# Output projection, residual and router by blocks of columns with the samples in them, smaller first weight tiles, and a new order of the work ahead of them, in a one-layer decoder step

## The chip, the cores and the metric

The kernel runs on one core of one Trainium2 chip. The metric is the device time of one execution in microseconds (us); three runs of the kernel before have a median of 1264.1 us. Engines are named as in the profile: PE is TensorE, DVE VectorE, ACT ScalarE, POOL GpSimd; SP only issues transfers (DMA).

## The reference

One layer of a decoder for a prompt of 256 tokens and 8 sample sequences of one token each, width 1024, everything in fp32:

```python
sh1, sc1, g1, sh2, sc2, g2 = jnp.split(jax.nn.silu(c) @ ada_w + ada_b, 6, axis=-1)
h = rms_norm(x, norm1_w) * (1.0 + sc1[:, None]) + sh1[:, None]
z = h @ w_in
...
x = x + g1[:, None] * (jnp.concatenate([ret_out, att_out], axis=-1) @ w_out)
h = rms_norm(x, norm2_w) * (1.0 + sc2[:, None]) + sh2[:, None]
ff = moe(h.reshape(B * T, D), router_w, router_b, w_gate_up, b_gate_up, w_down, b_down).reshape(B, T, D)
x = x + g2[:, None] * ff
```

`ret_out` is a retention (linear attention) group of 8 heads, `att_out` a sparse attention of 8 heads, which for the samples gathers the 256 best of 1024 cached keys and values. `moe` has 32 experts, of which each token takes the best 4; an expert is a gate-up matrix of 1024 x 2048, a clamped SwiGLU and a down matrix of 1024 x 1024, 12.58 MB in fp32. All 32 are read once, 402.7 MB.

## The kernel before

The program is one stream, in which a scheduler orders the instructions of every engine by the priority of the segment that they stand in: `seg("name")` opens a segment, and the table `PRIO` gives each name an offset. Pools of tiles add waits where a buffer is used again.

Ahead of the experts come: the conditioning (`ada`, six parts of 1024 columns, from `ada_w`), the input projection (`zblock`, blocks of 512 columns of `w_in`), the attention of the samples in two passes of four samples (`sample_attention(0)` and `(1)`: gathers of keys by POOL, scores by DVE, gathers of values by POOL (L895), probabilities times values on PE (L965), and the fold into `mixT` through L972 and L973), the retention, and then the output projection. `mixT` (128 x 8 x 288) holds the mixed heads with the width on the partitions; columns 0 to 255 are the prompt, 256 to 263 the samples.

The output projection `out_proj(c, k0)` makes, for a chunk `c` of 128 tokens, two blocks of 128 x 512 in two halves of the sum (`k0` is 4, then 0): 64 matmul instructions in all at L1277 (an fp32 matmul is two instructions in the profile), each block followed on DVE by a product with `g1b` (L1279) and a sum into `x` (L1280). The samples have matmuls of their own (L1285). After its projection a chunk is normed by `norm2(c)`: transposes into `xT` (which is `mixT`) and squares on ACT; then `router(c)`: 8 logit matmuls (L1353), the choice of the best 4 on DVE, and `ranks(c)`, each token's place among an expert's. Chunk 0 goes through this while PE still projects chunk 1. `keep_warm` puts 11 bf16 matmuls of no use (L1345) into the pauses of that stretch. `gather_in` (L1391) then collects the tokens of the first pair of experts by one-hot matmuls, DVE scales them (L1402), and expert 0 begins (gate-up L1581, transposes L1514, down L1591, scatter L1525).

Weights come through a ring of tiles, filled by SP in the order of use as tiles come free: 7 tiles of 2 MB (`ring2`), 4 of 1 MB (`ringp`), and, once `mixT` and its neighbours are free, one of 2 and one of 1 MB, 21 MB in all. The four tiles of `ringp` hold `w_out` (4 MB) first. So all but the last 7 MB of the ring is filled while the mixing still runs, and tile n of the second round is requested when the first round's tile n has been read. The first tile of the ring is thus freed by expert 0's first quarter.

Of the kernel before, what the change touches and what calls it, by code (L numbers as in the profile page):

```python
# [1793 lines left out]
```

## Time and profile before

| | us |
|---|---|
| median of three runs (1260.33, 1264.1, 1264.23) | 1264.1 |
| the profiled execution, its own time | 1260.99 |
| its span in the trace | 1259.2 |
| PE busy | 1171.8 (93%) |
| DVE busy | 488.6 (39%) |
| first matmul of the output projection's main part (L1277) | at 300.26 |
| first matmul of expert 0 (L1581) | at 347.27 |

The span is 1.8 us shorter than that execution's time. Times within the span count from its start. [...] In a timeline a bracket behind a group tells how long the engine was idle before it and what ended that.

### The profile page before, as it was taken

The numbers are of one execution on the slowest core, as the hardware profiler recorded it, in microseconds if no ns is written. First come the engines' busy times: TensorE is split into PE (matmuls) and PEld (weight loads), VectorE is DVE, ScalarE is ACT, GpSimd is POOL, SyncE is SP. The second block draws the span as 40 slices with busy tenths as digits, with TensorE's granted clock in tenths as the row PEclk, the third lists the DMA queues.
The fourth block names the chain that finished last, engine by engine and source line by source line (L and its number), as shares of the span: only waits on it lengthen the run. The fifth ranks groups of instructions, "written<-read, shape, count | busy, mean of one in ns | idle before, by whom it ended". The sixth has DMA issues, their size and how long they took to land. (4 is left out here: it accounts for less than half of the span.)

```text
span 1259.2 us, 14226 instructions
## 1 busy us (share of the span) xinstructions
PE 1171.8 (93%) x5672; PEld 467.3 (37%) x5673; DVE 488.6 (39%) x1171; ACT 134.5 (11%) x289; POOL 138.8 (11%) x221
## 2 busy tenths in 40 slices
PE   7999978889999999999999898989999898998998
PEld 3443333356533334333343333333333333333332
DVE  3239865436534233332333233232323232333243
ACT  1222112211210000000000000000000000000000
POOL 3402273340010000000000000000000000000000
PEclk8999999999999999999999999999999999999999
DMA  9636896757779999999999999999999999999997
GB/s 379 269 128 237 301 367 227 233 191 305 321 292 428 427 430 428 428 430 426 430 428 430 430 426 429 431 428 428 431 428 429 430 427 431 428 429 406 427 428 313
DMA packets 53350, 475.81 MB, mean 378 GB/s; under 512 B 6896, under 2 KB 7568, under 8 KB 15520
## 3 DMA queue, kind: packets, MB, share of 16 engines
q1 hardware_dynamic: 45472, 454.04, 86.2%
q0 software_dynamic: 4432, 13.74, 3.0%
q10 hardware_dynamic: 3376, 7.09, 1.8%
q8 instruction: 46, 0.75, 0.2%
q14 instruction: 24, 0.20, 0.0%
HBM read 470.69 MB, written 4.11 MB: 377 GB/s over the span
## 5 line engine op out<-in xcount | busy, mean ns | idle before, releaser
L1581 PE MATMUL pg<-w,xg 128*64 128x512 f32 x2048 | 470.6, 600 | 35.2 <-DMA w<-lay_w_exp 33.7
L1581 PEld LDWEIGHTS pg<-w,xg 128*64 128x64 f32 x2048 | 140.7, 137 | 322.0 <-issue 267.3
L1591 PE MATMUL py<-w,sg 128*64 128x512 f32 x1024 | 236.0, 602 | 11.9 <-DMA w<-lay_w_exp 11.4
L1555 DVE TENSOR_TENSOR hb<-pt,biasT 128x512 f32<-128x512 f32 x64 | 44.3, 692 | 358.9 <-PE pt L1514 350.2
L1540 POOL TENSOR_SCALAR og<-kp,rankm,comb 128x64 f32<-128x64 f32 (+1 forms) x64 | 36.9, 593 | 848.9 <-PE pz L1525 794.6
L1591 PEld LDWEIGHTS py<-w,sg 128*64 128x64 f32 x1024 | 71.0, 138 | 146.9 <-issue 129.7
L1547 ACT ACTIVATE hs<-pg 128x512 f32<-128x512 f32 x64 | 38.2, 597 | 614.5 <-PE pg L1581 614.5
L538 PE MATMUL acc<-w,hT 128*128 128x512 f32 x208 | 102.3, 623 | 0.0
L1598 DVE TENSOR_TENSOR ys<-py,g2n 64x512 f32<-64x512 f32 x62 | 42.7, 688 | 113.3 <-PE py L1591 112.6
L1525 PE MATMUL pz<-ys,og 128*128 128x512 f32 (+1 forms) x136 | 67.8, 630 | 1.6 <-DVE ys L1594 0.8
L1528 DVE TENSOR_TENSOR x<-x,pz 128x512 f32<-128x512 f32 x68 | 46.5, 688 | 58.2 <-PE pz L1525 58.2
L1391 PE MATMUL pz<-oh,hn 128*128 128x112 f32 x480 | 58.1, 274 | 0.0
L1391 PEld LDWEIGHTS pz<-oh,hn 128*128 128x128 f32 x480 | 56.0, 192 | 0.0
L538 PEld LDWEIGHTS acc<-w,hT 128*128 128x128 f32 x208 | 37.5, 196 | 42.5 <-issue 40.6
L1560 ACT ACTIVATE sg<-hb 128x256 f32<-128x256 f32 x64 | 26.7, 416 | 224.9 <-DVE hb L1559 224.9
L1514 PEld LDWEIGHTS pt<-ident,hs 128*128 128x128 f32 x256 | 27.0, 141 | 53.2 <-issue 53.2
L1514 PE MATMUL pt<-ident,hs 128*128 128x128 f32 x256 | 42.2, 287 | 0.0
L1525 PEld LDWEIGHTS pz<-ys,og 128*128 128x128 f32 (+1 forms) x136 | 23.1, 192 | 46.0 <-issue 29.6
L1577 DVE COPY og<-pt 128x256 f32<-128x256 f32 (+1 forms) x17 | 7.2, 424 | 63.8 <-PE pt L1514 63.8
L1563 DVE TENSOR_TENSOR sg<-sg,hb 128x256 f32<-128x256 f32 x64 | 26.9, 420 | 3.9 <-DVE hb L1562 0.5
L1562 DVE SCALAR_TENSOR_TENSOR hb<-hb 128x256 f32<-128x256 f32 x64 | 27.2, 425 | 2.2
L316 PE MATMUL acc<-w,cT 128*32 128x512 f32 x128 | 24.9, 609 | 0.5 <-ACT t L848 0.5
(461 smaller groups left out, 849.5 us busy)
## 6 DMA issues: line engine op xcount, KB each, us to landing
w<-lay_w_exp SPq DMA_DIRECT2D x130, 2048.0 KB, 28.1
w<-lay_w_exp SPq DMA_DIRECT2D x122, 1024.0 KB, 26.9
w<-lay_ada_w SPq DMA_DIRECT2D x20, 1024.0 KB, 10.9
w<-lay_w_in SPq DMA_DIRECT2D x15, 1024.0 KB, 6.5
w<-lay_w_out SPq DMA_DIRECT2D x4, 1024.0 KB, 5.4
s<-qd ACTq DMA_DIRECT2D x4, 512.0 KB, 7.8
w<-lay_w_exp SPq DMA_DIRECT2D x4, 512.0 KB, 14.8
hT<-lay_x SPq DMA_DIRECT2D x1, 1152.0 KB
```

The source lines that it names most:

```text
L538: T.matmul(pc[c], hT[:, k, 128 * c:128 * c + 128], w[k], start=(k == 0), stop=(k == 7))
L1391: put(T.matmul(px[:, k, :n, 8:64], hn[:, c, 512 * g + 128 * k:512 * g + 128 * k + 128], oh, start=(c == 0 and k == 0), stop=(c == 1 and k ...
L1514: on_pe(T.transpose(out, in_, ident[:k, :k]))
L1525: on_pe(T.matmul(pz[n], gT[i, 128 * c:128 * c + 128], ys[i, o:o + 512], start=True, stop=True))
L1528: V.tensor_add(x[:, c, sl], x[:, c, sl], pz[n])
L1540: G.tensor_scalar(og[:, c, js], iota2[:, 0:js.stop - js.start], rank(c), gate(c), op0=ALU.is_equal, op1=ALU.mult)
L1547: S.activation(hss[h], pg[h], AF.Copy)
L1555: V.tensor_tensor(hb, pt.rearrange("p (q b t) -> p q b t", q=4, b=2), bias.rearrange("p (b h q) -> p h q b", b=2, h=2)[:, h, :, :, None].t ...
L1562: V.scalar_tensor_tensor(up, up, 1.0, gate_, op0=ALU.add, op1=ALU.mult)
L1581: on_pe(T.matmul(pg[h][64 * b:64 * b + 64, :], xg[:, k, :], w[u][:, 512 * b:512 * b + 512], start=(k == 0), stop=(k == 7)))
L1591: on_pe(T.matmul(py[64 * n:64 * n + 64, :], sgs[k // 4][:, k % 4], w[u][:, 512 * n:512 * n + 512], start=(k == 0), stop=(k == 7)))
L1598: V.tensor_mul(ys[i64, 512 * n:512 * n + 512], py[64 * n:64 * n + 64], g2n[64 * n:64 * n + 64])
```

## The change

1. The projection goes by 8 blocks `m` of 128 output columns. `w_out` is the stationary side now, and `mixT` with prompt and samples (264 columns) the moving one: 64 matmuls of 128 x 264 in two halves, 128 instructions. DVE multiplies by the gate and adds in one instruction for the prompt and makes a small product for the samples. The result is `xT`, the transposed residual, read from the input in that form; `x` comes back from it by 16 transposes.
2. The logits of a block come right after the block; the squares follow in three groups of blocks (`rows`). Norm and router of both chunks stand after the whole projection. `keep_warm` is gone, and with it the projection of the samples by themselves, `g1b`, `srow`, 12 small transfers of POOL and 4 of ACT. The samples' norm is worked on POOL (`norm2_samples`), their logits come after the gathers in the program's text, and their residual is transposed during expert 11 (`sample_residual`).
3. The ring's first four tiles hold 1 MB instead of 2, and there are nine instead of seven in `ring2`: 4 x 1 and 5 x 2 MB. Its whole size stays 21 MB. The tile for the output bias (`output_bias`) is asked for after expert 9 instead of after expert 1.
4. `keep_busy`: 9 and 5 bf16 matmuls of no use ahead of and behind a transposition early in the program (in the words of the change, constants multiplied in first waits).
5. The table `PRIO` has new numbers, which moves work on all engines between the conditioning and the projection.

The diff, cut to its core:

```diff
-    "AB": -400, "AB0": -1600, "AB1": 200, "Sst": 800, "ada0_0": 100, "ada0_1": 0, "ada1_0": -400, "ada1_5": 100, "ada2_0": -800,
+    "AB": -400, "AB0": 800, "AB1": 200, "Sst": 20, "ada0_0": 100, "ada0_1": 0, "ada1_0": -400, "ada1_5": 100, "ada2_0": -20,
...
+    def keep_busy(n):
+        for i in range(n):
+            pe0(T.matmul(idle.rearrange("p (n m) -> p n m", n=4), ones_b, ones_b[:, None, :].to_broadcast([128, 4, 128]), start=True, stop=True))
...
+        if h == 0:
+            pe0(ins)
+            seg("wm")
+            keep_busy(9)
...
+    seg("wm")
+    keep_busy(5)
     seg("ikg")
...
-    ring2 = [ctx.enter_context(pool(f"ring2_{i}")) for i in range(RING2)]
+    ring2 = [(ctx.enter_context(pool(f"ring2_{i}")), 2 if i < 4 else 4) for i in range(RING2 + 2)]
...
-    nc.sync.dma_start(x, A["x_prompt"][0].rearrange("(c p) d -> p c d", p=128))
+    xT = prep.tile([128, 8, 264], F32, name="xT")
+    nc.sync.dma_start(xT, L["x"][:, :, 0:264])
...
+    def out_proj(m, k0):
+
+        seg(f'op{m}{k0}')
         ks = range(k0, k0 + 4)
...
+            T.matmul(pc[:, :264], wot[k][:, 128 * m:128 * m + 128], mixT[:, k, 0:264], start=(k == k0), stop=(k == k0 + 3))
+        V.scalar_tensor_tensor(xT[:, m, 0:256], pc[:, :256], condT[:, 0, m, 0:1], xT[:, m, 0:256], op0=ALU.mult, op1=ALU.add)
+        V.tensor_mul(ts[:, m], pc[:, 256:264], condT[:, 0, m, 1:9])
+        if m == 7:
+            G.tensor_add(xsT, xT[:, :, 256:264] if k0 else xsT, ts)
...
+    def rows(i, m0, m1):
+
+        seg(f'n2{i}')
+        w = 128 * (m1 - m0)
+        for c in range(2):
+            sl = slice(128 * m0, 128 * m1)
             pt = trp()
+            for m in range(m0, m1):
+                transpose(pt[:, 128 * (m - m0):128 * (m - m0) + 128], xT[:, m, 128 * c:128 * c + 128])
+            S.activation(hn[:, c, sl], pt[:, :w], AF.Square, accum_out=ss[:, c, i:i + 1])
+            V.tensor_copy(x[:, c, sl], pt[:, :w])
...
+    def logits(m):
+
+        seg(f'lo{m}')
+        for c in range(2):
+            T.matmul(pls[c][:, 0:32], xT[:, m, 128 * c:128 * c + 128], rwm[:, m], start=(m == 0), stop=(m == 7))
...
-    out_proj(2, 0)
-    out_proj(0, 0)
-    norm2(2)
...
-    norm2(0)
-    out_proj(1, 0)
-    router(2)
+    pls = [pm_.tile([128, 512], F32, name="py"), thp()]
+    for m in range(8):
+        out_proj(m, 0)
+        logits(m)
+        if m in (3, 5, 7):
+            rows(m // 2 - 1, (0, 4, 6)[m // 2 - 1], m + 1)
+    norm2()
     router(0)
+    router(1)
     pr = smp()
     ranks(0)
+    ranks(1)
     norm_rows(0)
-    keep_warm(WARM2[0], 0)
-    norm2(1)
-    keep_warm(WARM2[1], 1)
-    router(1)
-    keep_warm(WARM2[2], 2)
+    norm_rows(1)
+    norm2_samples()
...
-        if e == 1:
+        if e == 9:
             output_bias()
+        if e == 11:
+            sample_residual()
```

What the new table moves is seen on PE at the second pass of the samples' attention. In the kernel before, PE has these rows from the first pass's values (`kg` with `s_1508`) on; blocks of `w_in` (L538, L541) and the retention of the samples (L838) follow, and the second pass (`s_1716`) comes some 25 rows later:

```order
L965 MATMUL th<-kg,s_1508 32x512 x8
L548 MATMUL sm<-t_1779,kp 32x128 x4
L538 MATMUL acc<-w,hT 128x512
L972 MATMUL th<-kt,s_1532 128x4 x4
L538 MATMUL acc<-w,hT 128x512
L1083 MATMUL tr<-ident,ada 128x64 x4
L538 MATMUL acc<-w,hT 128x512 x3
...
L960 MATMUL th<-av_x,s_1716 128x512
L965 MATMUL th<-kg,s_1716 32x512
L270 MATMUL tr<-ident,t_1946 128x128 x4
L965 MATMUL th<-kg,s_1716 32x512 x7
```

In the changed kernel the same engine has this from the first pass's values (`s_1519`) to the second's (`s_1727`):

```order
L973 MATMUL th<-kg,s_1519 32x512 x8
L551 MATMUL sm<-w,hT 32x512
L980 MATMUL th<-kt,s_1543 128x4 x4
L274 MATMUL th<-ident,sk 128x128 x2
L945 MATMUL th<-qkn,qx 32x1 x16
L551 MATMUL sm<-w,hT 32x512 x7
L274 MATMUL th<-ident,ss__1711 128x128 x2
L274 MATMUL th<-ident,s_1721 128x128
L968 MATMUL th<-av_x,s_1727 128x512
L973 MATMUL th<-kg,s_1727 32x512 x8
```

The second pass has moved ahead of the blocks of `w_in` and stands 9 rows behind the first; the value gathers of POOL are issued in the same order as before.

On SP the transfers of the ring stood like this from `w_out` to the second round (`lay_w_exp` of 128x4096 is 2 MB, of 128x2048 is 1 MB; `in_b_down` and the `adad` behind it are the output bias):

```order
L167 DMA w<-lay_w_out 128x2048 x2
L167 DMA w<-lay_w_exp 128x4096 x2
L167 DMA w<-lay_w_out 128x2048 x2
L167 DMA w<-lay_w_exp 128x4096 x5
L167 DMA w<-lay_w_exp 128x2048 x4
L167 DMA w<-lay_w_exp 128x4096
L167 DMA w<-lay_w_exp 128x2048
L167 DMA w<-lay_w_exp 128x4096
L167 DMA w<-lay_w_exp 128x2048
L1640 DMA w<-in_b_down 32x1024
L341 DMA w<-adad 32x2x512
```

and stand like this in the changed kernel:

```order
L170 DMA w<-lay_w_out 128x2048 x2
L170 DMA w<-lay_w_exp 128x2048 x4
L170 DMA w<-lay_w_out 128x2048 x2
L170 DMA w<-lay_w_exp 128x4096 x5
L170 DMA w<-lay_w_exp 128x2048 x4
L170 DMA w<-lay_w_exp 128x4096
L170 DMA w<-lay_w_exp 128x2048 x5
L170 DMA w<-lay_w_exp 128x4096 x5
```

Of the `x5` in the seventh row one is the ring's last tile and four open the second round; the output bias has left this place.

On PE, at the end of the projection, the kernel before has this from the last logits of chunk 1 to expert 0 (L1581), where the gather of chunk 1 (`g1b`) comes last:

```order
L1353 MATMUL pt<-rwp,mixT 128x32 x4
L1345 LDWEIGHTS ones_b
L1345 MATMUL py<-ones_b 128x512
...
L1391 MATMUL pz<-ones_f,hn 128x2x56 x8
...
L1391 MATMUL pz<-g1b,hn 128x2x56 x7
L1581 MATMUL pg_2681<-w,xg 64x512 x16
```

and the changed one, from the last matmuls of the projection (L1279) to its first gather (L1380; the samples' logits are L1344):

```order
L1279 MATMUL pz<-mixT,w 128x264 x3
...
L1334 MATMUL pg_2442<-rwp,xT 128x32 x3
L274 MATMUL pt<-ident,xT 128x128 x2
L1334 MATMUL py<-rwp,xT 128x32 x3
L1334 MATMUL pg_2442<-rwp,xT 128x32 x3
L274 MATMUL pt<-ident,xT 128x128 x4
L1314 MATMUL pg_2587<-rss,ones_f 128x8
L1364 LDWEIGHTS tri_b
L1364 MATMUL pg_2571<-selb,tri_b 128x32
L1344 MATMUL pt<-rw__2353,h2Ts 8x32 x8
L1380 MATMUL pz<-ones_f,hn 128x2x56 x8
```

The samples' logits stand ahead of the first gather here, the matmuls of no use are gone, and 12 of the 16 logit matmuls and 8 of the 16 transposes come behind the last matmul of the projection.

## Rows read from the trace of the kernel before

**Rows 1.** The page: what the DMA engines moved in each of 40 slices of the span, in GB/s.

```profile
GB/s 379 269 128 237 301 367 227 233 191 305 321 292 428 427 430 428 428 430 426 430 428 430 430 426 429 431 428 428 431 428 429 430 427 431 428 429 406 427 428 313
```

**Rows 2.** Three stretches of the span: bounds and length in us, busy time (and count) of PE, of PE's weight loads, of DVE, ACT and POOL, PE's granted clock, the DMA engines' busy share, GB/s.

```profile
334.00:347.00 13.00, 11.48 (x100) 9.50 (x99) 7.84 (x41) 3.70 (x7) 2.00 (x6) 1.00 0.88 364
370.00:400.00 30.00, 29.81 (x146) 11.26 (x143) 11.07 (x23) 2.03 (x4) 0.00 (x0) 1.00 1.00 426
400.00:600.00 200.00, 200.00 (x937) 75.52 (x937) 69.02 (x140) 15.08 (x30) 8.96 (x16) 0.99 1.01 429
```

**Rows 3.** The same view in steps of 5 us around the start of expert 0.

```profile
345.00:350.00 5.00, 4.32 (x28) 2.63 (x29) 3.23 (x9) 0.00 (x0) 3.28 (x5) 1.00 0.06 23
350.00:355.00 5.00, 5.00 (x26) 1.93 (x24) 0.00 (x0) 0.60 (x1) 0.00 (x0) 1.00 0.61 220
355.00:360.00 5.00, 5.00 (x26) 1.85 (x24) 2.04 (x5) 1.70 (x2) 0.00 (x0) 1.00 0.98 416
360.00:365.00 5.00, 5.00 (x31) 2.40 (x28) 0.69 (x1) 0.60 (x1) 0.00 (x0) 1.00 0.59 193
365.00:370.00 5.00, 5.00 (x30) 2.32 (x30) 3.53 (x7) 0.42 (x1) 0.00 (x0) 1.00 0.87 334
```

**Rows 4.** SP's queue: issues from 346 us on (start, length from the first to the last of a group, count).

```profile
350.95 3.76 SPq L167 DMA_DIRECT2D w<-lay_w_exp  x2
358.57 0.34 SPq L1640 DMA_DIRECT2D w<-in_b_down  x1
```

**Rows 5.** The page's list of DMA issues: the experts' tiles of 2 MB and of 1 MB, with their count, size and median time from issue to landing in us.

```profile
w<-lay_w_exp SPq DMA_DIRECT2D x130, 2048.0 KB, 28.1
w<-lay_w_exp SPq DMA_DIRECT2D x122, 1024.0 KB, 26.9
```

**Rows 6.** PE's timeline between 213 and 262 us: start, length, what, and in brackets the idle time before it with what ended it.

```profile
213.49 1.92 PE L965 MATMUL th<-kg,s 128*32 128x512 f32 x16
...
221.96 0.43 PE L1083 MATMUL tr<-ident,ada 64*128 64x64 f32 x4 [3.53 <-DVE mixT L973]
...
245.70 0.43 PE L548 MATMUL sm<-t,kp 128*32 128x128 f32 x8 [0.78 <-ACT t L546]
...
247.58 0.33 PE L270 MATMUL th<-ident,s 128*128 128x128 f32 x1 [1.08 <-DVE s L951]
249.00 0.66 PE L270 MATMUL tr<-ident,t 128*128 128x128 f32 x4 [1.09 <-DVE t L512]
...
256.45 0.39 PE L972 MATMUL th<-kt,s 128*128 128x4 f32 x2 [0.86 <-DVE s L969]
...
260.15 2.42 PE L1184 MATMUL th<-s,qb 128*32 128x512 f32 x3 [2.42 <-DVE s L1024]
```

**Rows 7.** POOL's timeline: the gathers of the second pass's values, the first and the last of eight.

```profile
214.85 0.95 POOL L895 DMA_INDIRECT kg<-in_cache_v,rowi  x1 [17.69 <-PE th L965]
...
227.25 0.95 POOL L895 DMA_INDIRECT kg<-in_cache_v,rowi  x1 [0.30 <-issue]
```

**Rows 8.** The view of line L895: the time from a gather's issue to its landing, of all gathers of keys and values.

```profile
DMA to landing us min/median/max: 3.5/5.8/9.9
```

**Rows 9.** PE's timeline between 270 and 326 us: the last block of `w_in` (L558, 288 moving columns), the samples' projection (L1285) and one run of the prompt's (L1277).

```profile
270.21 8.51 PE L558 MATMUL acc<-hT,w 128*128 128x288 f32 x34
...
286.18 1.07 PE L1285 MATMUL sm<-w,mixT 128*32 128x256 f32 x16
...
295.71 1.07 PE L1285 MATMUL sm<-w,mixT 128*32 128x256 f32 x16
...
315.31 7.03 PE L1277 MATMUL pz<-w,mixT 128*128 128x512 f32 x16
...
322.70 1.48 PE L1285 MATMUL pg<-w,mixT 128*32 128x256 f32 x18
...
324.70 1.06 PE L1285 MATMUL pg<-w,mixT 128*32 128x256 f32 x14
```

**Rows 10.** PE's timeline from the first matmul of the projection's main part to expert 0.

```profile
300.26 6.28 PE L1277 MATMUL acc<-w,mixT 128*128 128x512 f32 x14 [0.51 <-DVE t L1164]
...
331.39 1.88 PE L1277 MATMUL pz<-w,mixT 128*128 128x512 f32 x4
...
333.36 1.97 PE L1353 MATMUL pt<-rwp,mixT 128*128 128x32 f32 x16
...
336.75 1.09 PE L270 MATMUL pt<-ident,x 128*128 128x128 f32 x8 [0.27 <-DVE lg L1360]
...
339.23 1.06 PE L1353 MATMUL pt<-rwp,mixT 128*128 128x32 f32 x8
...
340.77 1.93 PE L1391 MATMUL pz<-ones_f,hn 128*128 128x112 f32 x16
...
347.27 9.66 PE L1581 MATMUL pg<-w,xg 128*64 128x512 f32 x44 [0.68 <-POOL accs L1666]
```

**Rows 11.** DVE: the choice of the best 4 for chunk 1, its first and its last instruction ahead of the count, from the timeline.

```profile
340.33 0.25 DVE L1358 SCALAR_TENSOR_TENSOR lg<-pt,rinv,rbm 128x32 f32<-128x32 f32 x1 [0.88 <-PE pt L1353]
...
341.34 0.18 DVE L1366 TENSOR_SCALAR selb<-lg 128x32 bf16<-128x32 f32 x1
```

**Rows 12.** Two stretches in which the clock differs, columns as in Rows 2.

```profile
244.00:250.10 6.10, 3.15 (x25) 1.22 (x19) 4.16 (x8) 1.85 (x4) 3.82 (x6) 1.00 0.70 253
250.10:253.50 3.40, 3.40 (x8) 0.90 (x6) 1.78 (x4) 0.00 (x0) 1.21 (x4) 0.50 1.02 433
```

More of the change, by code (lines that the diff above doesn't have):

```diff
@@ L283, in hybrid_step @@
     idle = thp()
-    for i in range(WARM):
-        T.matmul(idle.rearrange("p (n m) -> p n m", n=4), ones_b, ones_b[:, None, :].to_broadcast([128, 4, 128]), start=True, stop=True)
+    pe0 = chain()
+    def keep_busy(n):
+        for i in range(n):
+            pe0(T.matmul(idle.rearrange("p (n m) -> p n m", n=4), ones_b, ones_b[:, None, :].to_broadcast([128, 4, 128]), start=True, stop=True))
+    keep_busy(WARM)
     sw_ = pe.tile([128, 204], F32, name="sw_")
@@ L326, in ada_half @@
             for j in range(4):
[L327 removed]
+                ins = T.matmul(pa[32 * j:32 * j + 32, :256], cT[:, k, :], w[k][:, 256 * j:256 * j + 256], start=(k == 0), stop=(k == 7))
+        if h == 0:
+            pe0(ins)
+            seg("wm")
+            keep_busy(9)
         sl = slice(256 * h, 256 * h + 256)
@@ L342, in ada_prompt @@
                     adad[b - 1].rearrange("(j r) d -> r j d", r=32)[0:1, j:j + 2, :].to_broadcast([out.shape[0], 2, 512]))
-    def ada_sample(q, out, b, j):
-        for n in range(4):
-            r = 32 * (j + n // 2) + 1
-            q.dma_start(out(n), adad[b - 1, r:r + 8, 256 * (n % 2):256 * (n % 2) + 256])
     def fold(b, w, j0):
@@ L1077, in hybrid_step @@
     ada_rows_out(2)
-    for i, (b, j) in enumerate(((1, 2), (2, 0))):
+    for i, (b, j) in enumerate(((1, 0), (1, 2), (2, 0))):
         pt = trp()
@@ L1215, in hybrid_step @@
     h2Ts = lat.tile([128, 8, 8], F32, name="h2Ts")
+    xsT = lat.tile([128, 8, 8], F32, name="xsT")
     comb = lat.tile([128, 3, NE], F32, name="comb")
@@ L1223, in hybrid_step @@
     res = lat.tile([128, 512], F32, name="res")
-    rings[:] = [(p, 4) for p in ring2] + [(ringp, 2)] * RING
+    rings[:] = ring2 + [(ringp, 2)] * RING
     wq[0] = 0
@@ L1263, in hybrid_step @@
     G.tensor_mul(rwm, rw_, modT[:, 1, :, None].to_broadcast([128, 8, NE]))
[L1264 removed]
     rinv = prep.tile([128, 2], F32, name="rinv")
     selb = prep.tile([128, 3, NE], BF16, name="selb")
[L1269 to L1271 removed]
+    ts = prep.tile([128, 8, 8], F32, name="ts")
+    def out_proj(m, k0):
+        seg(f'op{m}{k0}')
         ks = range(k0, k0 + 4)
[L1273 to L1289 removed]
@@ new lines, in norm2_samples @@
+    def norm2_samples():
+        seg('n2s')
+        sq = prep.tile([128, 8, 8], F32, name="sqs")
+        G.tensor_mul(sq, xsT, xsT)
+        r = prep.tile([128, 2, 8], F32, name="rss")
+        V.tensor_reduce(r[:, 0], sq.rearrange("p m t -> p t m"), axis=AX.X, op=ALU.add)
+        pt = thp()
+        T.matmul(pt[:, :8], ones_f, r[:, 0], start=True, stop=True)
+        S.activation(r[:, 0], pt[:, :8], AF.Sqrt, bias=epsc, scale=1.0 / D)
+        V.reciprocal(r[:, 1], r[:, 0])
+        G.tensor_mul(h2Ts, xsT, r[:, 1:2].to_broadcast([128, 8, 8]))
+        G.tensor_mul(h2Ts, h2Ts, condT[:, 2, :, 1:9])
+        G.tensor_add(h2Ts, h2Ts, condT[:, 1, :, 1:9])
@@ L1336, in hybrid_step @@
     G.memset(selb, 0.0)
-    pe2 = chain()
-    def keep_warm(n, c):
-        seg(f"wm{c}")
-        t = pm_.tile([128, 512], F32, name="py")
-        for i in range(n):
-            pe2(T.matmul(t.rearrange("p (n m) -> p n m", n=4), ones_b, ones_b[:, None, :].to_broadcast([128, 4, 128]), start=True, stop=True))
+    def logits(m):
+        seg(f'lo{m}')
+        for c in range(2):
+            T.matmul(pls[c][:, 0:32], xT[:, m, 128 * c:128 * c + 128], rwm[:, m], start=(m == 0), stop=(m == 7))
     def router(c):
@@ L1349, in router @@
         rows = 128 if c < 2 else 8
-        pl = trp()
-        for k in range(8):
-            if c < 2:
-                pe2(T.matmul(pl[:, 0:32], xT[:, k, 128 * c:128 * c + 128], rwm[:, k], start=(k == 0), stop=(k == 7)))
-            else:
+        if c < 2:
+            pl = pls[c]
+        else:
+            pl = trp()
+            for k in range(8):
                 T.matmul(pl[:8, 0:32], h2Ts[:, k], rw_[:, k], start=(k == 0), stop=(k == 7))
@@ L1634, in spill, with sample_residual @@
         last[0] = None
+    def sample_residual():
+        pt = pm_.tile([128, 512], F32, name="pt", bufs=2)
+        for m in range(8):
+            n = m // 4
+            T.matmul(pt[64 * n:64 * n + 8, 128 * (m % 4):128 * (m % 4) + 128], xsT[:, m], ident, start=True, stop=True)
+        for n in range(2):
+            V.tensor_copy(res[64 * n:64 * n + 8], pt[64 * n:64 * n + 8])
     def output_bias():
@@ L1677, in hybrid_step, with between @@
     first[0] = chain()
+    def between(e):
+        if e == 0:
+            nxt[0] = hits(lambda c: rankm[:, c, 2:4], 2)
+        elif e == 1:
+            gather(xgs[1], nxt[0], 0)
+        if e:
+            gather_next(e)
     nothing = scatter = lambda c: None
```

114 lines of the change are left out of this document (27 added, 87 removed), and 22 rows, old and new, of the table PRIO.

## The prediction

> **What bounds the kernel now.** I read the page's line of GB/s first [rows 1]: from the 13th slice on, some 380 us into the span, the DMA engines move 426 to 431 GB/s in nearly every slice to the end; before that they move 128 to 379. So there are two stages. In the second the experts' weights set the pace: 12.58 MB at 429 GB/s are 29.3 us an expert. PE is as busy there (200 of 200 us from 400 to 600) only because it works off what the ring held [rows 2]. PE's share of the span, 93%, is therefore not the bound; a microsecond saved on PE behind 370 us is worth nothing. The end is the moment at which the stream becomes dense, plus the bytes that are still to come, plus a short end. What counts is when the dense stream begins.
>
> The second view is the windows of 5 us around the start of expert 0 [rows 3]. The ring has been filled at 345 us, and nothing can be fetched until expert 0 frees a tile: 23 GB/s from 345 to 350. Then come 220, 416, 193 and 334. Over the 25 us that is 5 x (23 + 220 + 416 + 193 + 334) = 5,930 KB, or 13.8 us at 429. 11.2 us of stream are lost. Expert 0 begins at 347.27 [rows 10]. Put as one dense stream it starts at 345 + 11.2 = 356.2; the 115 KB that landed before 350 still belong to the filling of the ring (0.3 us), so I take 356.5, that is 9.2 us behind the start of expert 0. SP's queue shows why [rows 4]: the first refill is issued at 350.95, 3.7 us behind expert 0's start, since a tile of 2 MB has to be read whole; and one of the next tiles goes to the output bias at 358.57, a quarter of a MB in a tile of 2 MB.
>
> So the change can move the end in two ways: E, the start of expert 0, and the distance from E to the dense stream.
>
> **The distance from E.** Gate-up takes 9.66 us for 44 instructions, 0.22 us each [rows 10]; 1 MB of weights is 8 of them, 1.76 us. With first tiles of 1 MB the first is free at E + 1.8 and each further MB 1.76 us later, or 0.596 MB/us, faster than the 0.429 that the DMA takes: from there on the stream need not pause. From the issue at 350.95 to 355 it moved 220 GB/s x 5 us = 1.10 MB, 2.6 us of dense stream in 4.05 us; so 1.5 us pass until it flows. That gives E + 3.3. The output bias moves out of the hole, where its 0.26 MB were moved for nothing, into the dense stream: 0.6 us. Sum E + 3.9 against E + 9.2: **-5.3 us**. The bounds are -3.5 (the next tile waits once more for PE, 1.76 us) and -7 (the stream flows at once). Smaller transfers need not be slower: tiles of 1 MB make up 122 of the 252 large issues [rows 5], and the mixture runs at 429.
>
> **The output projection.** The nearest row to the new matmuls is the last block of `w_in` with 288 moving columns: 34 instructions in 8.51 us, 0.250 each [rows 9]; for 264 columns 0.229, times 128 is 29.4 us. The old form: 16 instructions in 7.03 us, 0.439 each, times 64 is 28.1 us. The samples go for nothing: 1.07 + 1.07 ahead of S, the start of the projection's main part at 300.26, and 1.48 + 1.06 within it. Within it that is 29.4 - 28.1 - 2.5 = -1.2; 4 of the 16 logit matmuls come to stand in it, at 1.97 us for 8 [rows 10], +1.0; the samples' norm leaves it, some -0.7. Sum -0.9. Ahead of S it is -2.1, and +0.4 for four more transposes of the conditioning, by the row at 221.96 [rows 6]. DVE has less to do a block (one instruction in place of two) and hides behind PE.
>
> **The order ahead of it.** Between 213 and 262 PE idles 3.53 + 0.78 + 1.08 + 1.09 + 0.86 + 2.42 = 9.8 us [rows 6], each time behind DVE or ACT: behind the fold at 221.96, in the second pass of the samples' attention, and in the retention of the samples. The new order puts that second pass right behind the first. For PE its waits then fall together with another one. The second pass's values are gathered into tiles that the first pass must have read: the first gather went out 1.4 us behind the first value matmul (214.85 against 213.49), the last at 227.25 [rows 7]. Without the wait for another transfer in their midst, eight gathers at 1.25 us with that transfer's 1.1 put the last at 1.4 + 8.8 + 1.1 = 11.3 us behind, and it lands 5.8 later [rows 8], at 17. Until then PE has the rows between the passes, by the like rows of before about 7.7 us, and the second pass's own 1.9, less the last matmul: it reaches the last tile at about 9.2. So PE waits about **8 us**, for which nothing stood in the trace of before, since blocks of `w_in` lay between the passes. DVE and ACT go on meanwhile, so I let all of the 9.8 us go. Bounds: none go and the wait is 12 (a gather that lands after 9.9 us [rows 8]), +12; or all go and the wait is 3, -7. I take -9.8 + 8 = -1.8, nearer to the gain because each of those six waits is for an engine that the new wait lets catch up. The 14 matmuls of `keep_busy` lie in waits of the first 25 us, at nothing; PE waits for other engines once more behind them.
>
> S moves by -2.1 + 0.4 - 1.8 = -3.5.
>
> **The end of the projection to E.** The last matmul of the projection ends at 333.27, expert 0 begins at 347.27: 14.0 us [rows 10]. In this stretch the change loses overlap, since both chunks are normed and routed behind the whole projection. From the logits of chunk 1 (339.23 + 1.06 = 340.29) to expert 0 the old one needs 7.0 us with one router. The new one: 8 transposes at 1.09 us for 8, and 12 logits at 1.97 for 8, make 4.1 us on PE; DVE's last block and the squares of the last group some 1.4 more; then those 7.0 with the other chunk's choice on DVE in between (340.33 to 341.52, 1.2 us [rows 11], with the rows behind it some 2), one more gather of 1.93, and the samples' logits ahead of it, 0.6. Sum 17.0, **+3.0 us**. The bounds are 14 (the chains of two chunks hide in each other) and 18.5. All of this was hidden behind chunk 1's projection in the kernel before; this is the price of the new form.
>
> **Sum.** E moves by -3.5 - 0.9 + 3.0 = -1.4, the dense stream by -1.4 - 5.3 = -6.7 us, and the end with it: nothing behind it changes but work on an engine that leads. 1260.99 - 6.7 = 1254.3 for an execution like the profiled one. That one is 3.1 us below the median of three; which of them a run of the changed kernel is like, no row shows, so I add half: **1256**.
>
> [...]
>
> **The rivals.**
> - *The clock falls in the new pauses.* The two chunks' gathers, 1.93 us each, take twice as long in part, about +1.9, and expert 0's first MB 3.5 us in place of 1.76: +3.6 in all, 1259.6. For it: the pauses behind the choice on DVE. Against: 4 us of transposes and logits stand shortly ahead.
> - *The order gives nothing back.* The wait for the values is there, and half of the old waits stay: E at +3.5, -1.8 in all, 1260.7.
> - *Slower.* The second pass's values land late (12 us of wait), the old waits stay and the end of the projection takes 18.5: E moves by -2.1 + 0.4 + 12 - 0.9 + 4.5 = +13.9, less 5.3 is +8.6: 1271. The point from which it decides is E at +5.3, where the gain of the smaller tiles is used up; to be measurably slower (1267.9, below) it takes E at +10.7. For it: the gathers' row shows the serial POOL and nothing lies in between now. Against: it needs the late landing and none of the waits to go.
> - *The order gives more.* The gathers land in time for all but 3 us of wait: 1251; with a shorter end of the projection, 1248.
> - *The tiles do nothing,* because the stream waits for something else than the first tile (a register or semaphore on SP): then only E counts, 1261. I hold it for unlikely, since SP's first issue follows the first tile's last matmul by 0.2 us [rows 4, 10].
>
> **How the numbers follow.** Forecast 0.41, clock 0.13, order gives nothing 0.18, slower 0.11, more 0.14, tiles do nothing 0.03. A difference below 0.3%, 3.8 us, is one that a measurement of this kernel can hardly tell from none: faster is below 1260.3, slower above 1267.9. The forecast counts as faster for 0.38 of its 0.41, "more" whole, the clock for 0.08, "nothing" for 0.07: 0.66 with rounding. Slower are 0.10 of the slower case and 0.02 of the others: 0.12. The same 0.22. The range leaves out the late landing and the best end of "more": 1247 to 1266.
>
> **What would show it.** SP issues the first refill within 2 us of expert 0's first matmul, and the windows behind it reach 420 GB/s within 5 us: right on the tiles. PE idles 5 to 10 us behind POOL's gathers at the second pass's value matmuls, and the other five waits between the passes and the retention are gone: right on the order. From the projection's last matmul to expert 0 it takes 16 to 18 us, with the granted clock at 1.00: right on its end. Wrong it would be if E moved later by more than 5 us, if the stream had holes behind E + 4, or if the dense part ran below 425 GB/s.

## The result, and the profile after

The changed kernel takes **1281.8 us** (median of 4 runs, 1273.75 to 1284.08), the kernel before 1264.2 (4 runs beside them): a ratio of 1.0131, interval 1.0102 to 1.0161. It is slower; 1256 was forecast, and the time lies above the range. The profiled execution after took 1280.75 us, its span is 1279.0: 19.8 us more than before.

The page's line of GB/s after, to be laid beside [rows 1]:

```profile
GB/s 378 265 84 241 287 362 239 206 181 297 341 354 422 424 425 422 424 424 391 424 424 425 423 423 424 425 423 423 425 423 424 423 426 424 422 408 360 424 422 289
```

From the 13th slice on, where 426 to 431 stood, stand 422 to 426, and three slices ahead of the last are low: the 19th (391), the 36th (408) and the 37th (360), where 426, 429 and 406 stood. Stretches of the trace after, columns as in [rows 2]; the first five answer to [rows 3]:

```profile
345.00:350.00 5.00, 4.19 (x21) 3.91 (x20) 2.29 (x9) 0.00 (x0) 1.56 (x3) 0.50 0.34 141
350.00:355.00 5.00, 4.96 (x19) 2.64 (x20) 2.44 (x8) 0.00 (x0) 0.69 (x2) 0.60 0.00 0
355.00:360.00 5.00, 5.00 (x26) 1.85 (x24) 0.00 (x0) 0.00 (x0) 0.00 (x0) 1.00 0.81 311
360.00:365.00 5.00, 5.00 (x28) 1.78 (x25) 1.61 (x4) 1.27 (x2) 0.00 (x0) 1.00 0.97 349
365.00:370.00 5.00, 5.00 (x28) 1.74 (x26) 0.45 (x2) 1.63 (x3) 0.00 (x0) 1.00 1.01 421
400.00:600.00 200.00, 200.00 (x950) 75.80 (x948) 68.87 (x139) 15.21 (x30) 8.97 (x16) 1.00 1.01 424
600.00:620.00 20.00, 17.70 (x77) 7.19 (x74) 9.39 (x18) 1.01 (x2) 0.00 (x0) 0.92 1.02 373
640.00:1100.00 460.00, 426.53 (x1990) 160.61 (x1988) 144.68 (x295) 31.56 (x63) 17.62 (x32) 0.99 1.01 424
1135.00:1140.00 5.00, 4.48 (x22) 1.32 (x24) 2.04 (x5) 0.42 (x1) 0.00 (x0) 1.00 0.95 369
1140.00:1160.00 20.00, 18.31 (x85) 7.43 (x83) 8.39 (x16) 1.01 (x2) 2.33 (x4) 1.00 0.77 305
```

The same view of the kernel before, of the three late stretches that its rows above don't hold:

```profile
640.00:1100.00 460.00, 422.85 (x1959) 156.94 (x1956) 141.60 (x289) 32.01 (x63) 17.92 (x32) 0.99 1.01 429
1135.00:1140.00 5.00, 4.21 (x14) 1.50 (x10) 3.77 (x6) 0.00 (x0) 0.00 (x0) 1.00 0.77 306
1140.00:1160.00 20.00, 17.43 (x77) 6.27 (x76) 3.57 (x9) 1.61 (x3) 2.33 (x4) 0.95 1.01 423
```

Where the 19.8 us went can be read from these. **The start of the dense stream:** from 355 to 370 it moved 5 x (311 + 349 + 421) = 5,405 KB, 12.75 us at 424, so it starts at 357.25, against 356.5 before: 0.75 us. **Its rate:** the 902.7 us that the kernel before needs from there to its span's end become 902.7 x 429/424, 10.6 us more; the busy share of the DMA engines is 1.01 in both, so they don't wait, they move fewer bytes in the same busy time. **600 to 620:** 373 instead of 424 costs 20 x (1 - 373/424) = 2.4 us; the output bias stands there now, 0.26 MB in a tile for 2 MB. **1135 to 1160:** here is the only branch behind the router, ahead of expert 28 (`spill`, for an expert that has over 56 tokens), and SP issues nothing across it for a while: from 1142.2 to 1155.6 us here, from 1127.0 to 1138.0 before. Missing are 0.65 + 5.61 = 6.3 us of stream after, 1.43 + 0.28 = 1.7 before: 4.6 us. Together 18.4 of 19.8.

PE's timeline after, the rows that answer to [rows 6] and [rows 10], and one stretch of the clock:

```profile
209.29 1.92 PE L973 MATMUL th<-kg,s 128*32 128x512 f32 x16
...
214.37 1.05 PE L980 MATMUL th<-kt,s 128*128 128x4 f32 x8 [2.20 <-DVE s L977]
...
219.19 0.41 PE L274 MATMUL th<-ident,ss__1711 128*128 128x128 f32 x2 [1.39 <-DVE ss__1711 L957]
...
221.93 2.69 PE L973 MATMUL th<-kg,s 128*32 128x512 f32 x6
224.99 4.06 PE L973 MATMUL th<-kg,s 128*32 128x512 f32 x10 [0.37 <-DMA kg<-in_cache_v,rowi]
...
238.93 0.46 PE L1090 MATMUL tr<-ident,ada 64*128 64x64 f32 x4 [1.24 <-DVE condT L1091]
...
261.41 1.12 PE L274 MATMUL tr<-ident,t 128*128 128x128 f32 x4 [5.30 <-DVE t L522]
...
301.55 5.61 PE L1279 MATMUL acc<-mixT,w 128*128 128x264 f32 x24
...
331.77 1.50 PE L1279 MATMUL pz<-mixT,w 128*128 128x264 f32 x6
...
342.61 3.76 PE L1380 MATMUL pz<-ones_f,hn 128*128 128x112 f32 x16
...
347.23 2.90 PE L1380 MATMUL pz<-oh,hn 128*128 128x112 f32 x12 [0.81 <-DVE oh L1373]
...
351.91 10.70 PE L1561 MATMUL pg<-w,xg 128*64 128x512 f32 x44
```

```profile
342.60:346.20 3.60, 3.60 (x19) 3.56 (x18) 1.21 (x6) 0.28 (x1) 0.81 (x2) 0.50 0.98 414
```

The projection starts at 301.55 and ends at 331.77 + 1.50 = 333.27, to the hundredth where it ended before. From there to expert 0 it takes 18.64 us against 14.0, and the 16 matmuls of the first gather take 3.76 us for 1.93: at 342.6 to 346.2 the granted clock is 0.50, where it was 1.00 from 334 to 347 [rows 2]. So expert 0 starts 4.6 us later than in the profile before, a run that differs from this one already at 70 us (see the order ahead of the projection, below); and nevertheless the dense stream starts only 0.75 us late, since SP's first refill now follows expert 0's start by 3.0 us and the stream by 5.3 (9.2 before):

```profile
354.91 13.09 SPq L170 DMA_DIRECT2D w<-lay_w_exp  x6
```

What is least expected is the rate of the whole stream behind it. The page's list of issues after:

```profile
w<-lay_w_exp SPq DMA_DIRECT2D x98, 2048.0 KB, 26.3
w<-lay_w_exp SPq DMA_DIRECT2D x186, 1024.0 KB, 24.6
```

The change touches that stream in three ways: 4 of the 9 tiles of `ring2` have 1 MB, where all 7 had 2, so that 186 of its issues are of 1 MB (122 in [rows 5]); the bias stands at another place; and in the pool of lasting tiles, which lies ahead of the ring in SBUF, `xs` and `modT` (1024 + 64 bytes a partition) have given way to `condT` (864), so that `ring2` begins 224 bytes lower, at byte 50720 of a partition in place of 50944. 50944 is a multiple of 256, 50720 lies 32 bytes behind one.

### The profile page after: what moved, and what is told of

It reads as the page before. It is cut to its first block, busy times and chain, and to the rows that moved or that the text cites. A ratio compares the mean times of both kernels' runs of the same rounds, so it can differ in the third digit from the quotient of the medians.

```text
span 1279.0 us, 14344 instructions
## 1 busy us (share of the span) xinstructions
PE 1187.0 (93%) x5693; PEld 486.1 (38%) x5694; DVE 489.5 (38%) x1186; ACT 133.1 (10%) x288; POOL 134.5 (11%) x212
## 5 line engine op out<-in xcount | busy, mean ns | idle before, releaser
L1561 PE MATMUL pg<-w,xg 128*64 128x512 f32 x2048 | 476.6, 607 | 39.4 <-DMA w<-lay_w_exp 38.3
L1571 PE MATMUL py<-w,sg 128*64 128x512 f32 x1024 | 238.6, 607 | 8.2 <-DMA w<-lay_w_exp 6.8
L1380 PE MATMUL pz<-oh,hn 128*128 128x112 f32 x496 | 62.1, 280 | 0.8 <-DVE oh L1373 0.8
L1380 PEld LDWEIGHTS pz<-oh,hn 128*128 128x128 f32 x496 | 59.6, 197 | 0.9 <-DVE oh L1373 0.9
```

The costliest lines, as they stand in the source:

```text
L1380: put(T.matmul(px[:, k, :n, 8:64], hn[:, c, 512 * g + 128 * k:512 * g + 128 * k + 128], oh, start=(c == 0 and k == 0), stop=(c == 1 and k ...
L1561: on_pe(T.matmul(pg[h][64 * b:64 * b + 64, :], xg[:, k, :], w[u][:, 512 * b:512 * b + 512], start=(k == 0), stop=(k == 7)))
L1571: on_pe(T.matmul(py[64 * n:64 * n + 64, :], sgs[k // 4][:, k % 4], w[u][:, 512 * n:512 * n + 512], start=(k == 0), stop=(k == 7)))
```

## The experiments

Each ratio is to the kernel before on the same chip, with its 95% interval; the rates are those of the stretch 640 to 1100, which holds neither bias nor branch, in the one profiled execution of a version.

**e1: the kernel before with the change's tiles.** The first theory, A, was that the smaller transfers slow the stream.

```diff
-    ring2 = [ctx.enter_context(pool(f"ring2_{i}")) for i in range(RING2)]
+    ring2 = [(ctx.enter_context(pool(f"ring2_{i}")), 2 if i < 4 else 4) for i in range(RING2 + 2)]
...
-    rings[:] = [(p, 4) for p in ring2] + [(ringp, 2)] * RING
+    rings[:] = ring2 + [(ringp, 2)] * RING
```

> The kernel before with the ring of the change alone (4 tiles of 1 MB, 5 of 2 MB in front; the output bias stays behind expert 1). Theory A, that transfers of 1 MB cost the stream more per byte than those of 2 MB: the windows from 400 to 1100 us show about 424 GB/s in place of 429, which is 10 us over some 375 MB; the hole behind expert 0's start is some 4 us smaller; the time is 1268 to 1274. Rival B, that the lower rate comes from something else in the changed kernel: 429 GB/s, and with the smaller hole 1258 to 1262.

1268.51 (10 runs), ratio 1.0045 (1.0022 to 1.0067), and 428 GB/s. The tiles alone cost time, a third of what the change costs, but hardly by the rate; f5 takes up where else.

**e2: the changed kernel with the old tiles** (that line the other way round).

> The changed kernel with the old ring (7 tiles of 2 MB in front), all else as in the change. A: the windows from 400 to 1100 us are back at 429 GB/s (10 us won), the first refill comes 3.5 us and more behind expert 0's start (some 4 us lost); 1272 to 1277. B: 424 GB/s as in the changed kernel, and only the hole grows: 1284 to 1288.

1273.99 (4 runs), 1.0099 (1.0066 to 1.0132), and 425 GB/s with the tiles of before: theory A falls. Expert 0 starts at 345.58 here.

**e4: all loads cut to 1 MB,** in the kernel before, in the same tiles.

```diff
-w = weights(L["w_exp"][e], (*range(0, 24, 2), 21, 23) if e == NE - 1 else ())
+w = weights(L["w_exp"][e], (*range(0, 24, 2), 21, 23) if e == NE - 1 else tuple(range(0, 24, 2)))
```

> The kernel before with every tile of 2 MB of the experts filled by two transfers of 1 MB (8 KB a row each); tiles and their release stay as they were. A: the share of bytes in 1 MB transfers goes from about 32% to 100%; if 16 points of share cost 5 GB/s, as between the two kernels, the windows from 400 to 1100 us show some 408 GB/s, and the time is 1295 to 1315. B: 429 GB/s and 1260 to 1268.

1269.66 (9 runs), 1.0055 (1.0032 to 1.0078), 426 GB/s. Twice the issues of half the size cost 0.7% of the rate; the 64 that the change adds can cost a tenth or two of a per cent by that (an estimate), which is what e1 shows (428 for 429).

**e5: each 2 MB load cut by rows,** two of 64 partitions in place of one of 128.

```diff
+for h in range(2):
+    load(w[64 * h:64 * h + 64, b - i:j - i], src[64 * h:64 * h + 64, b:j])
```

> The kernel before with every transfer of 2 MB of the experts cut in two by partitions: 64 rows of 16 KB each, so that the number of transfers grows as in the run with 1 MB transfers, and the row stays at 16 KB. A, if it is the length of a row that counts: 429 GB/s, 1260 to 1268. A', if it is the number of transfers: as slow as the run that cuts to rows of 8 KB. B: 429 GB/s.

2046.84 (4 runs), ratio 1.617 (1.6055 to 1.6284), 225 GB/s: half the rate. It says nothing on the size of packets, for which it was made. Two loads of 64 partitions each, issued in turn, ran at half the rate of one load of 128 (225 GB/s for 429), with the DMA engines' busy share at 0.98 for 1.01. Why is not shown.

Rows of these four, 640 to 1100, in the order e1, e2, e4, e5:

```profile
640.00:1100.00 460.00, 425.06 (x1966) 158.14 (x1962) 141.48 (x289) 31.41 (x62) 17.99 (x32) 0.99 1.01 428
```

```profile
640.00:1100.00 460.00, 421.44 (x1978) 157.23 (x1976) 142.75 (x291) 31.42 (x62) 18.00 (x32) 1.00 1.01 425
```

```profile
640.00:1100.00 460.00, 426.63 (x1960) 153.39 (x1958) 142.50 (x291) 30.99 (x62) 17.91 (x32) 1.00 1.01 426
```

```profile
640.00:1100.00 460.00, 285.62 (x1018) 98.35 (x1020) 72.59 (x149) 16.21 (x32) 9.00 (x16) 0.79 0.98 225
```

**e6 to e8, the place of the tiles.** The second theory, C in the texts below: the 224 bytes, that is, the place of the tiles within a partition, told by multiples of 256 or of 64 bytes. Its rival D: the place is of no matter. The kernel before gets an unused tile of 32 bytes in the lasting pool (e6), the changed one 32 (e7, tiles 64 bytes behind a multiple of 256) or 224 (e8, `[128, 56]`, the place of before).

```diff
+    per.tile([128, 8], F32, name="shift")
```

> The kernel before with an unused tile of 32 bytes a partition in front of the 2 MB tiles: in the two programs these start at byte 50944 of a partition (a multiple of 256) before and at 50720 (32 beyond a multiple of 64) in the change; here at 50976. Nothing else is touched. [...] Rival D, that the place is of no matter and the changed kernel's rate comes from elsewhere (the place of the weights in HBM, the chip): 429 GB/s and the time of the kernel before.

> The changed kernel with an unused tile of 32 bytes a partition, so that the tiles start at 50752 and on, on a multiple of 64 but not of 256. C with 256 bytes: 424 GB/s and the time of the changed kernel, 1276 to 1284. C with 64 bytes: 428 GB/s and some 9 us less. D: 424 GB/s.

> The changed kernel with an unused tile of 224 bytes a partition: the tiles start at 50944 and on, multiples of 256, as in the kernel before. C (256 or 64 bytes): 428 GB/s as in the old kernel with the small tiles, and 8 to 11 us less than the changed kernel, 1268 to 1274. D: 424 GB/s, no gain.

e6: 1272.12 (5 runs), 1.0066 (1.0041 to 1.0091), 425 GB/s. 32 unused bytes make the kernel before 0.7% slower. e7: 1278.88 (4), 1.0117 (1.0079 to 1.0155), 424: multiples of 64 don't mend it. e8: 1270.06 (5), 1.007 (1.0041 to 1.01), 428: 224 bytes do, and take back 0.6 of the 1.31%.

**e9: all tiles of the ring at multiples of 256.** In the kernel before, `ringp` lies 128 bytes and the two late tiles 64 bytes behind one. If every tile off the boundary pays as `ring2` does in e6 (4 GB/s for 14 of the 21 MB), the other 7 MB have some 2 GB/s to gain, an estimate.

```diff
+    ctx.enter_context(pool("shift0")).tile([128, 32], F32, name="shift0")
...
+    per.tile([128, 32], F32, name="shift")
...
-    mp.tile([128, 176], F32, name="pad")
+    mp.tile([128, 192], F32, name="pad")
```

> The kernel before with unused tiles of 128, 128 and 64 bytes a partition, so that all tiles of the ring start on multiples of 256 (before it was those of ring2, 14 of 21 MB; the tiles of ringp stood 128 bytes beyond, ringx and ringy 64). [...] C with 64 bytes, or D: 429 GB/s and the time of the kernel before.

1262.76 (10 runs), 0.9982 (0.9964 to 0.9999), 429 GB/s, as before. The rest of the ring pays little or nothing for its place. This is the one version whose whole interval lies below 1, by less than the 0.3% that this kernel lets one tell.

**e10: the changed kernel, aligned (as e8), with the bias behind expert 1** (`if e == 1` for `if e == 9`). **e11: as e7, with the tiles 128 bytes behind a multiple of 256** (`[128, 24]`). **e12: as e10, with 11 warm matmuls between the router's steps,** eight behind the last transposes and three ahead of the samples' logits. **e13: as e10, with the old tiles,** so that only the new order and form of the projection are left.

> The changed kernel with its tiles on multiples of 256 (as in the run shifted by 224 bytes) and with the output bias behind expert 1 again. If the bias behind expert 9 costs what the trace of the change shows at 600 us (373 GB/s over 20 us in place of 424, 2.4 us of stream), that dent is gone, the early refill of a 1 MB tile is used for the bias, and the time is 1 to 3 us below that run: a ratio to the kernel before of 1.003 to 1.007. Rival: the bias costs the same wherever it is asked for, ratio as there, 1.007.

> The changed kernel with an unused tile of 96 bytes a partition: the tiles start at 50816 and on, odd multiples of 128. If boundaries of 128 bytes count (which would be why aligning the kernel before to 256 gained so little: there only ringx and ringy stood off 128), 428 GB/s and a ratio to the kernel before of 1.005 to 1.009. If boundaries of 256 bytes count, 424 GB/s and 1.011 to 1.016.

> As the run with aligned tiles and the early bias, and with 11 bf16 matmuls of no use in the pauses behind the projection (8 behind the last transposes, 3 ahead of the samples' logits). If it is the clock at 0.50 from 342 to 353 us that makes the gathers take 3.8 us in place of 1.9 and expert 0 start late: clock 1.00 there, gathers 1.9 us each, expert 0 some 4 us earlier behind the projection's last matmul (14 to 15 in place of 18.6), and 3 to 5 us less than that run. Rival: the pauses come back elsewhere or the stream's beginning doesn't follow expert 0, 0 to 1 us.

> The changed kernel with the old ring, aligned, and the early bias: only the projection by blocks, the serial norm and router and the new order of the work are left of the change. If these are what my prediction took them for (expert 0 1.4 us earlier), ratio to the kernel before 0.997 to 1.001. If the lost overlap and the clock behind the projection cost what the trace of the change shows (expert 0 4.6 us later), 1.002 to 1.005.

e10: 1272.23 (12 runs), 1.006 (1.0035 to 1.0085). The dent at 600 is gone (426 GB/s there), but the time can't be told from e8's: from 400 to 580 us, where e8 moves 428 GB/s, e10 moves 419, which is 3.8 us of stream (its cause is not shown). e11: 1278.96 (6), 1.0109 (1.0081 to 1.0137), 424: half of 256 does not do. e12: 1270.65 (12), 1.0034 (1.0011 to 1.0057); the clock fell all the same (below), the first gather again took 3.76 us, and expert 0 came at 354.97. e13: 1267.45 (12), 1.0036 (1.0016 to 1.0056), 429. The windows of e12 around its gathers:

```profile
343.00:348.00 5.00, 4.30 (x31) 3.40 (x31) 2.42 (x13) 1.68 (x3) 2.72 (x8) 0.60 0.99 421
348.00:353.00 5.00, 4.19 (x21) 3.97 (x20) 2.30 (x9) 0.00 (x0) 1.50 (x3) 0.50 0.28 120
```

**f1 and f2, which tiles are meant.** The kernel before with the 32 bytes directly ahead of `ring2` (f1, so that only `ring2` and what lies above it shift) or directly behind it (f2).

```diff
+    ctx.enter_context(pool("shift")).tile([128, 8], F32, name="shift")
```

> The kernel before with an unused tile of 32 bytes a partition directly in front of the 2 MB tiles: only these and the small tiles behind them (norms, router results) move, by 32 bytes. If the place of the 2 MB tiles is the cause: 425 GB/s and a ratio to the kernel before of 1.005 to 1.009, as in the run with the pad further ahead. If it was one of the tiles between (the experts' biases, the residual x): 429 GB/s and 1.000.

> The kernel before with the same 32 bytes directly behind the 2 MB tiles: only the small tiles behind move. If the place of the 2 MB tiles is the cause: 429 GB/s, ratio 1.000. If it is the small ones that the engines read and write during the experts: 425 GB/s.

f1: 1269.48 (10 runs), 1.0062 (1.0038 to 1.0086), 425. f2: 1265.56 (10), 0.9994 (0.9971 to 1.0016), 429. It is the place of the `ring2` tiles and nothing that lies below or above them. The same stretch of e6, e8, e9, f1 and f2:

```profile
640.00:1100.00 460.00, 419.88 (x1946) 156.13 (x1942) 141.58 (x289) 31.42 (x62) 17.91 (x32) 0.99 1.01 425
```

```profile
640.00:1100.00 460.00, 430.54 (x2035) 163.40 (x2033) 147.50 (x302) 32.85 (x65) 17.92 (x32) 0.99 1.01 428
```

```profile
640.00:1100.00 460.00, 422.80 (x1968) 157.81 (x1966) 143.37 (x293) 31.54 (x63) 17.91 (x32) 1.00 1.01 429
```

```profile
640.00:1100.00 460.00, 418.81 (x1938) 155.80 (x1936) 140.23 (x286) 31.00 (x61) 17.92 (x32) 0.99 1.01 425
```

```profile
640.00:1100.00 460.00, 424.31 (x1984) 159.35 (x1979) 142.59 (x291) 32.02 (x63) 17.91 (x32) 1.00 1.01 429
```

**f4 and f5, where the small tiles' gain goes.** The kernel before without the branch (f4), and e1 without it (f5).

```diff
-            first[0] = None
-            spill(xgs[1])
-            first[0] = chain()
...
```

> The kernel before without the code for experts with over 56 tokens and its branch ahead of expert 28 (with this input the branch is not taken; the computation loses that case). The dent to 365 GB/s at 1135 us is gone, 1.7 us of stream: ratio to the kernel before 0.997 to 1.000.

> The old kernel with the small first tiles, without that code and branch (the computation loses the case of over 56 tokens an expert). If the longer hole at the branch is what made the small tiles lose, they win here: 4.5 us of hole less, 2 us of rate (428 for 429) lost, ratio to the old kernel without the branch 0.997 to 0.999. If they lose for another reason, the ratio stays at 1.003 to 1.005.

f4: 1265.31 (10 runs), 1.0008 (0.9983 to 1.0033). f5: 1266.49 (10), 1.0014 (0.9991 to 1.0036). Without the branch the small tiles cost nothing that can be told, and still bring nothing; e1's interval and f5's overlap, so that the times alone don't settle what the branch adds. Their stretch 345 to 375, f4 and then f5:

```profile
345.00:375.00 30.00, 29.39 (x154) 13.11 (x156) 11.65 (x25) 3.31 (x5) 3.22 (x5) 1.00 0.70 272
```

```profile
345.00:375.00 30.00, 29.49 (x155) 13.08 (x156) 11.65 (x25) 3.31 (x5) 3.22 (x5) 1.00 0.85 324
```

Expert 0 starts at 347.76 and 347.40. 324 against 272 over 30 us are 1.56 MB, 3.6 us of stream, which f5 has ahead there; between their times, 0.06% apart the other way (0.7 us, within the noise), nothing of it is left to see. 428 for 429 over the 880 us behind it are 2.1 us; where the rest went is not shown.

With the branch the hole there decides. These are e1's, e2's and e13's, 1140 to 1160:

```profile
1140.00:1160.00 20.00, 16.27 (x66) 6.41 (x67) 6.39 (x13) 1.01 (x2) 2.34 (x4) 1.00 0.80 326
```

```profile
1140.00:1160.00 20.00, 17.69 (x74) 6.00 (x72) 7.27 (x14) 1.02 (x2) 2.34 (x4) 1.00 0.77 307
```

```profile
1140.00:1160.00 20.00, 15.84 (x64) 5.28 (x65) 6.78 (x12) 0.00 (x0) 2.33 (x4) 1.00 0.94 390
```

4.8, 5.6 and 1.8 us are missing in them. The old ring with the bias early has the small hole; either the small tiles (e1) or the bias behind expert 9 (e2) make it the large one. So it is in every profile with the branch that keeps the sizes of the loads: from 1100 to 1170 us 1.1 to 1.8 us are missing with old ring and early bias (before, e6, e9, e13, f1, f2) and 4.9 to 6.3 in the eight others; e4, with all loads at 1 MB, has 3.3. That fits a branch that falls on another place in the ring's turn, with less of the stream issued ahead of it. It was argued from these runs, not tried by itself.

## Why the prediction was wrong

The step that failed is the last of the sum: "the end with it: nothing behind it changes but work on an engine that leads". The stream's own rate was carried over from the kernel before, and in the "smaller transfers" paragraph only the size of its transfers was weighed against it, not the place that they are written to. That place is not in the diff's words; it follows from which tiles stand ahead of the ring. Between the two profiles the end came 26.5 us later than forecast (+19.8 for -6.7): 17.6 of it lie behind the start of the dense stream (10.6 of rate, 2.4 at the bias, 4.6 at the branch) and 7.5 ahead of it (+0.75 for -6.7).

Told by parts, each from its own pair of runs: the place of `ring2` costs 0.62% (f1; 0.66% in e6, and 0.6% come back in e8), the small tiles with the branch 0.45% (e1), the new order and projection 0.36% (e13). The sum is 1.43%, measured are 1.31%, within the intervals; e2, which has the place and the order (and the late bias) without the small tiles, should have 0.98% and has 0.99%.

That an early start of the stream does not carry through to the end, e8's profile shows. Three of its windows:

```profile
345.00:375.00 30.00, 29.04 (x140) 10.71 (x141) 8.76 (x23) 3.31 (x5) 2.18 (x4) 1.00 0.86 347
1135.00:1140.00 5.00, 4.55 (x14) 1.67 (x13) 3.80 (x7) 0.00 (x0) 0.22 (x1) 1.00 0.31 128
1140.00:1160.00 20.00, 18.29 (x91) 7.08 (x89) 3.81 (x11) 2.02 (x4) 2.11 (x4) 1.00 0.96 395
```

There the stream is dense at 375 - 30 x 347/428 = 350.7, 5.8 us earlier than before (6.7 were forecast), and its rate is 428; but the span is 1262.3, 3.1 longer. Of these 8.9 us the rate takes 2.1, the bias 1.9 (346 GB/s from 590 to 600 us), and the larger hole at the branch 3.3.

What the prediction named as signs against it came: "the dense part below 425 GB/s" (424), and holes behind E + 4 (349 from 360 to 365 us). None of the rivals had the rate as a mechanism: the slower rival was a late E, and its point of decision, E at +5.3, was not reached (+4.6).

Point by point:

- **The distance from E to the dense stream** (-5.3 forecast). The mechanism was right: the first 1 MB tile comes free early and the stream is dense at E + 5.3 in place of E + 9.2, in a run in which the slow clock (0.50 and 0.60 from 345 to 355) held expert 0's first matmuls back (10.70 us for 44, 9.66 before); the forecast was E + 3.9. At the full clock it is about E + 4.3 (e8, e11), so -4.9. Its two halves don't add up: the late bias alone, with the old tiles, gives E + 5.3 (e2), the small tiles alone E + 5.0 and E + 5.9 (e1, f5). And the gain did not last: with the small tiles the stream runs at 428 for 429, and the branch's hole grows.
- **The bias** was moved out of one hole and made another (2.4 us in the profile after). "Into the dense stream: 0.6 us" was the bytes alone; a tile for 2 MB, held for 0.26 MB, was left out. e10 takes the dent away without a gain that can be told.
- **The output projection** (-0.9 forecast): 31.72 us from first to last matmul, 33.01 before, -1.3. Right.
- **The order ahead of it** (S, the start of the projection, moves by -3.5). The pair of profiles shows +1.3, but it is not a fair pair. From 70 to 110 us the granted clock is 1.00 in the profile before and 0.87 in the one after. The order and the clock can be told apart, since e2, with the new order, has 1.00 there, and e1, with the old one, 0.87 (before, after, e2, e1):

```profile
70.00:110.00 40.00, 37.26 (x199) 16.85 (x198) 23.43 (x77) 9.75 (x21) 6.29 (x9) 1.00 0.50 191
70.00:110.00 40.00, 37.37 (x183) 16.32 (x182) 19.47 (x63) 9.73 (x21) 5.74 (x8) 0.87 0.38 144
70.00:110.00 40.00, 37.24 (x200) 16.93 (x199) 24.14 (x78) 9.75 (x21) 6.32 (x9) 1.00 0.51 190
70.00:110.00 40.00, 37.36 (x184) 16.31 (x183) 19.33 (x63) 9.72 (x21) 5.73 (x8) 0.87 0.39 143
```

  The first pass's values, the projection's start, the first gather and expert 0 of e2, then of e1:

```profile
204.84 1.92 PE L973 MATMUL th<-kg,s 128*32 128x512 f32 x16
...
296.78 5.61 PE L1279 MATMUL acc<-mixT,w 128*128 128x264 f32 x24
...
337.84 3.76 PE L1380 MATMUL pz<-ones_f,hn 128*128 128x112 f32 x16
...
345.58 9.66 PE L1561 MATMUL pg<-w,xg 128*64 128x512 f32 x44 [0.52 <-DVE xg L1391]
```

```profile
218.04 1.92 PE L965 MATMUL th<-kg,s 128*32 128x512 f32 x16
...
305.21 6.28 PE L1277 MATMUL acc<-w,mixT 128*128 128x512 f32 x14 [0.51 <-DVE t L1164]
...
352.11 9.66 PE L1581 MATMUL pg<-w,xg 128*64 128x512 f32 x44 [0.58 <-DVE xg L1402]
```

  Over the profiles of either order (without e4 and e5, whose loads of 2 MB are cut in two): where the clock from 70 to 110 us is 1.00, S lies at 299.4 to 301.0 with the old order (before, e6, f1, f4, f5) and at 296.8 and 297.5 with the new one (e2, e8), -3.3 between means; where it is 0.79 to 0.87, at 305.2 to 308.0 (e1, e9, f2) and at 301.6 to 305.9 (the other six), -2.6. So S moved nearly as forecast, but not in the way forecast, and that is luck. The row of the second pass's value matmuls takes 2.69 + 0.37 + 4.06 us in place of 1.92, 5.2 more where I had 8; the waits that should have gone came back elsewhere, 2.20, 1.39, 1.24 and 5.30 us in the rows above, 10.1 for 9.8, the last behind DVE's rope (L522) of a chunk of the prompt. From the first pass's value matmuls to S it takes 6 us more at either clock; but those come 9 us earlier (204.8 and 205.6 for 213.5 to 215.2; 209.3 to 212.9 for 218.0 to 221.6), which the prediction did not have.
- **The end of the projection to E** (17.0). It is 17.1 in e2, e8 and e11, and 18.6 to 18.8 in the profile after and in four others. The 17.0 had both gathers at the full clock; but in all eight profiles of the new order the first gather takes 3.76 us for 1.93, so that 17.1 agrees only because the rest is 1.7 us shorter than forecast. In the five others the clock is down in the second gather too (0.50 from 347.2 to 350.2 in the profile after). So the first rival came true as to the clock, and its 18.9 is near what these five show. Before, 0.50 stood right behind a stretch in which PE was busy for 3.15 of 6.10 us [rows 12], and 1.00 from 334 to 347, where the matmuls of `keep_warm` lay in the pauses [rows 2]; now it is 0.50 behind the new pauses (342.6 to 346.2 in the profile after). That the pauses cause it is not shown here, and 11 warm matmuls at the places of e12 did not hold the clock (3.76 us again).
- **E as a whole** (-1.4). With the clock at 1.00 from 70 to 110 us E lies at 346.4 to 348.1 with the old order and at 345.6 and 346.3 with the new one: -1.4. With 0.79 to 0.87 it lies at 352.1 to 355.0 and at 351.9 to 356.2: +1.2. So nearly all of the 4.6 us between the two profiles goes with the early clock. It was down in six of the eight profiles of the new order and in three of the eight of the old one. That would fit e13, whose twelve times all lie above 1265, while 14 of the 29 of the kernel before on that chip lie below 1262; whether the new order brings it about is not shown.

The place of `ring2` shows in six profiles: 32, 64 and 128 bytes behind a multiple of 256 cost the same (425 GB/s in e2, e6 and f1, 424 in the profile after, e7 and e11, where 429 in the profile before and 428 in e8 were moved on one). The place of the other tiles hardly shows: by e6's price (4 GB/s and 0.66% for 14 MB) e9 should have gained some 2 GB/s and 0.3% for the other 7 MB, an estimate, and it gained none of the first and 0.2% of the second.

What stays open: why the place of `ring2` counts; why `ringp`, 128 bytes off in both kernels, pays little or nothing while `ring2` at 128 off pays in full (e11); whether other distances than these three pay too; and what exactly sizes the hole at the branch.
